# A two-layer RWKV-7 / gMLP trunk: a third plain pair in the first FFN, four weight splits moved from GpSimd to VectorE, and group norm's root by ScalarE

## The chip, the cores and the metric

The kernel runs on one core of a Trainium2 chip. A core has a matrix engine (TensorE, PE in the profile, with its weight loads as PEld), a vector engine (VectorE, DVE), an activation engine (ScalarE, ACT), GpSimd (POOL) and a queue engine that issues DMAs (SyncE, SP). The engines run their own instruction streams in order and wait for each other by semaphores. The metric is the device time of one execution in microseconds; lower is better.

## The reference, cut to what matters

Two layers on x (1 x 512 x 1024, float32). Layer 0 mixes with RWKV-7, layer 1 with a spatial gating unit (SGU). After each mixer comes a SwiGLU FFN of inner width 2816, and each sub-layer has a norm ahead and one behind.

```python
def _rmsnorm(x, g):
    y = x32 * lax.rsqrt(jnp.mean(x32 * x32, axis=-1, keepdims=True) + RMS_EPS)
    return (y * g.astype(jnp.float32)).astype(x.dtype)

def _rwkv7_time_mix(x, ...):
    ...
    y = _rwkv7_scan(r_h, decay.reshape(B, T, H, N), k_h, v_h, -kk, kk * a_h)
    mu = jnp.mean(y, axis=-1, keepdims=True)
    var = jnp.mean(jnp.square(y - mu), axis=-1, keepdims=True)
    y = (y - mu) * lax.rsqrt(var + GN_EPS)              # group norm, 16 heads of 64
    y = y * gn_w.reshape(H, N) + gn_b.reshape(H, N)
    y = y + jnp.sum(r_h * k_h * r_k, axis=-1, keepdims=True) * v_h
    return (y.reshape(B, T, D) * g) @ w_o

def _swiglu(x, w_gate, w_up, w_down):
    return (jax.nn.silu(x @ w_gate) * (x @ w_up)) @ w_down

def reference(x, ...):
    for i in range(DEPTH):                              # DEPTH = 2
        h = _rmsnorm(x, norm_gains[i, 0])
        h = _rwkv7_time_mix(h, ...) if i == 0 else _sgu_mixer(h, ...)
        x = x + _rmsnorm(h, norm_gains[i, 1])
        h = _rmsnorm(x, norm_gains[i, 2])
        h = _swiglu(h, ffn_w_gate[i], ffn_w_up[i], ffn_w_down[i])
        x = x + _rmsnorm(h, norm_gains[i, 3])
    return x
```

## The kernel before

**Products.** Every float32 operand of a large product is split in two parts of TensorE's fp32r type: `hi`, a cast by ScalarE (L179), and `lo`, the rest, a subtraction by VectorE (L180). `mm3` (L204) then issues three matmuls for each tile: hi by hi, hi by lo, lo by hi. `weight` loads a weight tile by SP's queue into one of two `wraw` buffers and splits it; with `pool=True` the cast is L195 and the rest is made by GpSimd (L196).

**Order.** The kernel is written as one program; the builder orders the instructions of each engine by a simulated timeline (`schedule_with_timeline_sim=True`), in which program order is the priority. So an instruction can stand ahead of one that is written before it, where the earlier one has to wait. Tiles come from pools with a fixed number of buffers. The pool `s` has 17 slots of 4 KB a partition, the pool `x` has 13: `hT` (8), the FFN's `act` tiles (11), `cc` and the operands of three products lie in `s`; the raw operands, the operands of the other four products and the weight sums lie in `x`.

**RWKV layer.** The work goes in four blocks of 256 features, each through projection (P), decay and key work (E), the front and back of a block inverse (F, B), a scan over 8 chunks (S) and the finish (N), in the order of the list PLAN: all E steps stand ahead of all N steps. In the scan (L1009 to L1024) TensorE, VectorE and ScalarE (su, Y) hand small tiles to each other. The finish is `group_norm` (L1038 to L1046): a mean, a variance by ScalarE's Square (L1042) and a reduction (L1044), then `rsqrt` (L214 to L223), which makes 1/sqrt by an integer guess and three Newton steps, twelve instructions of VectorE on 128x16 or 128x8, and the scaling of Y (L1046). It is called five times: for blocks 0 to 2 on all tokens, for block 3 on each half of them. Then TensorE transposes Y (yt, L1084), VectorE applies gn_w (L1085), TensorE makes the gate, VectorE multiplies (ob, L1089), and `ob` is split for the output projection.

**out_proj.** Output projection, the norm behind it, the residual and the transposes for the next norm. The result has two column halves of four token tiles; `post0` (L309) takes the squares' sum of the first half (L237) and applies the gain, `post1` (L317, L254 to L258, L320) does the same to the second half, takes the root by ScalarE's Sqrt and VectorE's correction, and adds to x. `norm.step` then transposes x (ptr, L267) and writes `hT` with its two parts, by ScalarE (L60) and VectorE (L62). After the RWKV layer (`spare` is set) post0 is called for each token tile just ahead of post1, and at the first of them a Sqrt of one column (L312) has ScalarE load that function's table early. Elsewhere it stands at the last token tile.

**FFN.** The 22 column tiles of gate and up go in 11 pairs. A plain pair (`plain`, L455 to L470) is two tiles by two weights by 8 k-tiles by three matmuls, 512 columns wide (for the first pair of each FFN two times 256); VectorE multiplies by the row of norms (L467) and by the up part (L469), ScalarE does SiLU (L468), GpSimd multiplies by the row again (L470). The other pairs go by a Strassen-like scheme (`Quads`, p1 to p7): seven products of 24 matmuls of 256 columns (R, Q, Z), on sums of weight quarters (`wsum`, L387) and seven prepared operands `bc` (L105 to L127, made by `quads.first` and `quads.second`). PLAIN = 2 pairs of each FFN are plain. They stand ahead, and the seven operands are made beside them. For the first four weight tiles of the first FFN, `weight` is called with `pool=j < 2`; in the second FFN the weights of its first two tiles come ready from the SGU.

```python
yb = plain(0, None)
quads = Quads(self, norm, yb)
quads.first()
for n in range(1, PLAIN):
    plain(n, yb)
p1(PLAIN); p2(PLAIN)
quads.second()
p1(PLAIN + 1); p2(PLAIN + 1)
for n in range(PLAIN, NJ // 2):
    for p in (p5, p6, p7, p3, p4) if n < PLAIN + 2 else (p1, p5, p6, p2, p7, p3, p4):
        p(n)
```

Of the kernel before, what the change touches and what calls it, by code (L numbers as in the profile page):

```python
# [7 lines left out]
F32 = mybir.dt.float32  # L8
F32R = mybir.dt.float32r
I32 = mybir.dt.int32  # L10
AF = mybir.ActivationFunctionType
ALU = mybir.AluOpType

P = 128
# [3 lines left out]
TT = T // P  # L18
# [4 lines left out]
NJ = DFF // P  # L23
RMS_EPS = 1e-6
GN_EPS = 64e-5
# [10 lines left out]
XV = "xxxessss"  # L36
XSLOTS = 13
LAG = 2
PLAIN = 2
DECAY = 0.5 * 0.6065306597126334  # L40


# [88 lines left out]
class Trunk:  # L131
# [77 lines left out]
    def rsqrt(self, ss, n, scale, eps):  # L209
# [13 lines left out]
            v.scalar_tensor_tensor(y, t, 1.5, y, op0=ALU.add, op1=ALU.mult)  # L223
        return y

    def bcast_row(self, row):

        t = self.gp.tile([P, D], F32, name="gain", tag="gain", bufs=2)
        self.nc.gpsimd.dma_start(out=t, in_=row.partition_broadcast(P))
        return t  # L230
# [42 lines left out]
    def out_proj(self, acts, wrows, nk, row, xts, store=None, tail=3, norm=None, spare=None, mid=None, after=()):  # L273


        nc = self.nc
        v = nc.vector
        gain = self.bcast_row(row)
        nu = nk // 2
        cols = [slice(0, 512), slice(512, 1024)]  # L280
        late = (1, 1) if spare else (0, tail)
        accs, f0, part = [None, None], [], []

        def mms(half, k, tt, w):
            tok = slice(tt * P, (tt + 1) * P)
            hi, lo = acts(k)
            self.mm3(accs[half][tt], (hi[:, tok], lo[:, tok]), w, k == 0, k == nk - 1)

        def unit(half, u):
            own = spare if half and u < nu - late[1] else None  # L290
            with ExitStack() as order:
                for ins in after:
                    order.enter_context(self.tc.issue_after(ins.ins))
                hi, lo = self.weight(wrows(u)[:, :, cols[half]], spare=own)
            return [(2 * u + j, (hi[:, j, :], lo[:, j, :])) for j in range(2)]

        def first(half):
            accs[half] = self.accs(half)
            for u in range(nu - late[half]):
                for k, w in unit(half, u):  # L300
                    for tt in range(TT):
                        mms(half, k, tt, w)

        def post0(tt, junk):
            acc = accs[0][tt]
            s = self.sumsq(acc, junk)
            if tt % 2 == 0:
                f0.append(self.f0p.tile([P, 2, 512], F32, name="f0", tag="f0", bufs=2))
            v.tensor_tensor(f0[-1][:, tt % 2, :], acc, gain[:, cols[0]], op=ALU.mult)  # L309
            part.append(self.part(s, 1.0 / D, RMS_EPS))  # L310
            if tt == (0 if spare else TT - 1):
                nc.scalar.activation(junk[:, 0:1], part[tt][0], AF.Sqrt)  # L312

        def post1(tt, hn):
            acc, lo, hi = accs[1][tt], hn[:, 0:512], hn[:, 512:1024]
            s = self.sumsq(acc, lo)
            v.tensor_tensor(hi, acc, gain[:, cols[1]], op=ALU.mult)  # L317
            y = self.rsqrt1(s, part[tt], 1.0 / D)
            for f, c in ((f0[tt // 2][:, tt % 2, :], cols[0]), (hi, cols[1])):
                v.scalar_tensor_tensor(xts[tt][:, c], f, y[:, 0:1], xts[tt][:, c], op0=ALU.mult, op1=ALU.add)  # L320
                if store is not None and tt == TT - 1:
                    nc.sync.dma_start(out=store[tt * P:(tt + 1) * P, c], in_=xts[tt][:, c])
            if store is not None and tt < TT - 1:
                nc.sync.dma_start(out=store[tt * P:(tt + 1) * P, :], in_=xts[tt])

        hn_tile = lambda: self.sm.tile([P, D], F32, name="hn", tag="hn", bufs=2)
        first(0)
        if not spare:
            for tt in range(TT):
                post0(tt, hn_tile()[:, 0:512])  # L330
        if mid:
            mid()
        first(1)
        ends = [[kw for u in range(nu - late[half], nu) for kw in unit(half, u)] for half in range(2)]
        for tt in range(TT):
            for half in range(2):
                for k, w in ends[half]:
                    mms(half, k, tt, w)
            if norm and tt >= LAG:
                norm.step(tt - LAG, xts[tt - LAG])  # L340
            hn = hn_tile()
            if spare:
                post0(tt, hn[:, 512:1024])
            post1(tt, hn)
        if norm:
            for tt in range(TT - LAG, TT):
                norm.step(tt, xts[tt])
            norm.finish()
# [5 lines left out]
    def ffn(self, li, xts, norm, store=None, nxt=None, early=()):  # L354
        nc = self.nc
        early = list(early)
        v, a = nc.vector, nc.scalar
        gains = self.i["norm_gains"]
        wgu = self.gate_up(li)
        wd = self.i["ffn_w_down"][li].rearrange("(u j p) n -> u p j n", p=P, j=2)  # L360
        hT, b = norm.hT, {}
        acts, pairs, loads, seeded = [], {}, [0], []
# [27 lines left out]
        def p1(n):  # L390
            o = pairs[n] = dict(act=self.slot([P, 2, T], F32, "act"))
            acts.append(o["act"])
            o["a11"] = quad(n, 0, 0)
            o["R"] = self.bank("R", "R")
            product(o["R"], 1, o["a11"], True)
            if len(seeded) < 2:
                q = self.bank("Q", "Q")
                seeded.append(q)
                bh = b[1][0]
                nc.tensor.matmul(q, bh[:, 0, 0:P], bh[:, 0:2].rearrange("p k t -> p (k t)"), start=True, stop=True)  # L400
            o["Q"] = seeded[(n - PLAIN) % 2]
            a.copy(o["Q"], o["R"])

        def gate(dst, src, sign=1.0):
# [7 lines left out]
        def p2(n):  # L412
            o = pairs[n]
            o["a12"] = quad(n, 1, 0)
            product(o["R"], 2, o["a12"])
            gate(o["act"][:, 0, g], o["R"])
# [36 lines left out]
        def plain(n, yb):  # L453
            act = self.slot([P, 2, T], F32, "act")
            acts.append(act)  # L455
            for f in range(2):
                j = 2 * n + f
                ws = early.pop(0) if early else [self.weight(w[:, :, j * P:(j + 1) * P], pool=j < 2) for w in wgu]
                pp = [self.bank("gu", "gu") for _ in range(2)]
                for c in ((g, u) if j < 2 else (slice(0, 512),)):  # L460
                    for w, ps in zip(ws, pp):
                        for kt in range(KT):
                            self.mm3(ps[:, c], (w[0][:, kt, :], w[1][:, kt, :]), (hT[kt][:, 0, c], hT[kt][:, 1, c]),
                                     kt == 0, kt == KT - 1)
                yb = norm.row() if yb is None else yb
                t = act[:, f]
                v.tensor_tensor(t, pp[0], yb, op=ALU.mult)  # L467
                a.activation(t, t, AF.Silu)  # L468
                v.tensor_tensor(t, t, pp[1], op=ALU.mult)  # L469
                nc.gpsimd.tensor_tensor(t, t, yb, op=ALU.mult)  # L470
            return yb
# [2 lines left out]
        quads = Quads(self, norm, yb)  # L474
        b = quads.b
        quads.first()
        for n in range(1, PLAIN):
            plain(n, yb)
        p1(PLAIN)
        p2(PLAIN)  # L480
        quads.second()
        p1(PLAIN + 1)
        p2(PLAIN + 1)
        for n in range(PLAIN, NJ // 2):
            for p in (p5, p6, p7, p3, p4) if n < PLAIN + 2 else (p1, p5, p6, p2, p7, p3, p4):
                p(n)

        halves = {}
# [41 lines left out]
    def rwkv(self, x0):  # L530
# [3 lines left out]
        with ExitStack() as ctx:  # L534
# [496 lines left out]
            def group_norm(Y, tts):  # L1031

                n, n4 = len(tts), 4 * len(tts)
                ts = slice(tts[0], tts[-1] + 1)
                y4 = Y[:, ts].rearrange("p t q (h v) -> p (t q h) v", h=2)
                yf = Y[:, ts].rearrange("p t q f -> p (t q f)")
                mu = self.sm.tile([P, n4], F32, name="mu", tag="mu", bufs=2)
                v.tensor_reduce(mu, y4, axis=mybir.AxisListType.X, op=ALU.add)  # L1038
                v.tensor_scalar(mu, mu, 1.0 / 64, None, op0=ALU.mult)
                v.tensor_tensor(y4, y4, mu.unsqueeze(2).broadcast_to([P, n4, C]), op=ALU.subtract)  # L1040
                sq = self.sm.tile([P, n4, C], F32, name="hn", tag="hn", bufs=2)
                a.activation(sq.rearrange("p q v -> p (q v)"), yf, AF.Square)  # L1042
                va = self.sm.tile([P, n4], F32, name="va", tag="va", bufs=2)
                v.tensor_reduce(va, sq, axis=mybir.AxisListType.X, op=ALU.add)  # L1044
                rs = self.rsqrt(va, n4, 1.0 / 64, GN_EPS)
                v.tensor_tensor(y4, y4, rs.unsqueeze(2).broadcast_to([P, n4, C]), op=ALU.mult)  # L1046

            def bonus(b, o):
# [244 lines left out]
```

## Time and profile before

| | us |
|---|---|
| median of 3 runs (lowest, highest) | 1354.4 (1348.42, 1357.36) |
| the profiled execution: time, span | 1345.89, 1344.2 |
| mean granted clock of TensorE | 0.979 |
| first FFN: first gate/up matmul, first R, last Q | 466.2, 519.9, 712.5 |
| second FFN: first R, last Q | 1033.9, 1219.4 |
| TensorE busy in 320 to 340, 360 to 380, 400 to 420 | 16.47, 15.61, 20.00 |

The span is from the first to the last instruction. A row of a timeline gives the start, the duration, the engine, the line, the operation, the tiles written and read, the shapes and the count; in brackets stand the engine's idle time ahead of it and what ended it. Busy times of TensorE are modelled, since matmuls are pipelined: 0.28 us stands for a 256-column matmul of which the next one starts after 0.12 us. So work is counted by matmuls and stretches. PEclk is the clock granted to TensorE, 1.00 for full speed. The lines that carry the argument are shown in the prediction.

### The profile page before, as it was taken

The page shows a single profiled execution, that of the slowest core. Times are in us where ns is not written, and L with a number is a line of the kernel's source. Part 1 is how long each engine was busy: PE and PEld are TensorE (multiplying, and loading weights), DVE is VectorE, ACT ScalarE, POOL GpSimd, SP SyncE. Part 2 cuts the span into 40 slices and gives each one's busy share as a digit, 9 for nine tenths or more (in the row PEclk, how much of TensorE's full clock was granted, in tenths as well). Part 3 has the DMA queues.
Part 4 walks back from the last instruction along what each step waited for, and adds up shares of the span by engine and source line. Part 5 has one row for each costly group of instructions (what it writes and reads, how often), then busy time and mean ns, then how long its engine had stood idle before and what let it go on. Part 6 is the DMA issues. An engine that isn't in the chain of part 4 may idle for free.

```text
span 1344.2 us, 24525 instructions
## 1 busy us (share of the span) xinstructions
PE 1279.7 (95%) x9812; PEld 1115.3 (83%) x9812; DVE 898.5 (67%) x1520; ACT 694.9 (52%) x1240; POOL 166.3 (12%) x306
## 2 busy tenths in 40 slices
PE   5999999988989799999999999999999999999997
PEld 3677799887767698899998887878888999998886
DVE  7975846667856589778775325575689878785223
ACT  7976884757443554445454314543464455464221
POOL 0000373665000121000000002020002000000000
PEclk9999999989889999999999999999999999999999
DMA  5146683412143233333323332343430443323231
GB/s 159 47 107 169 165 199 127 123 47 78 45 139 106 72 91 101 107 114 108 106 87 110 94 112 91 93 140 98 142 95 2 125 126 95 97 78 125 94 94 63
DMA packets 217266, 140.10 MB, mean 104 GB/s; under 512 B 67856, under 2 KB 193344, under 8 KB 217152
## 3 DMA queue, kind: packets, MB, share of 16 engines
q1 hardware_dynamic: 215856, 133.81, 34.6%
q0 software_dynamic: 1296, 4.72, 1.0%
q8 instruction: 77, 1.26, 0.4%
q14 instruction: 37, 0.30, 0.1%
HBM read 124.35 MB, written 14.16 MB: 103 GB/s over the span
## 4 chain that ended last, share of the span: by engine, by line
PE 58%; DVE 5%; ACT 1%; issue 1%; DMA 0%; SPq 0%; DVEq 0%; ACTq 0%
PE acc L204 24%; PE Q L204 11%; PE Z L204 7%; PE R L204 7%; PE gu L204 5%; PE u L204 3%; DVE wlo L180 1%; DVE wsum L387 1%; PE s L1227 1%; PE ptr L267 0%; ACT whi L179 0%; DVE braw L106 0%; DVE hT L62 0%; DVE bc L180 0%; DVE x L320 0%
## 5 line engine op out<-in xcount | busy, mean ns | idle before, releaser
L180 DVE TENSOR_TENSOR wlo<-wraw,whi 128x1024 fp32r<-128x1024 f32 x109 | 133.6, 1226 | 197.8 <-ACT whi L179 197.4
L179 ACT CAST whi<-wraw 128x1024 fp32r<-128x1024 f32 x109 | 114.2, 1048 | 224.1 <-PE acc L204 140.9
L204 PE MATMUL acc<-whi,actw 128*128 128x512 f32 x704 | 220.7, 394 | 0.0
L204 PE MATMUL Q<-bc,whi 128*128 128x256 f32 x864 | 157.2, 282 | 3.5 <-ACT hn L431 2.2
L204 PEld LDWEIGHTS acc<-whi,actw 128*128 128x128 f32 x704 | 132.3, 188 | 30.7
L204 PE MATMUL acc<-wlo,actw 128*128 128x512 f32 x352 | 138.7, 394 | 0.0
L204 PEld LDWEIGHTS Q<-bc,whi 128*128 128x128 f32 x864 | 133.8, 190 | 4.3 <-ACT hn L431 2.6
L179 ACT CAST whi<-wsum 128x1024 fp32r<-128x1024 f32 x72 | 75.2, 1050 | 90.3 <-PE Q L204 31.3
L204 PE MATMUL Q<-bc,wlo 128*128 128x256 f32 x432 | 121.7, 282 | 0.0
L204 PE MATMUL Z<-bc,whi 128*128 128x256 f32 x576 | 106.8, 283 | 0.0
L204 PE MATMUL R<-bc,whi 128*128 128x256 f32 x576 | 105.3, 281 | 0.8 <-ACT whi L179 0.8
L180 DVE TENSOR_TENSOR wlo<-wsum,whi 128x1024 fp32r<-128x1024 f32 x72 | 87.0, 1220 | 20.3 <-ACT whi L179 19.1
L204 PE MATMUL gu<-hT,whi 128*128 128x256 f32 (+1 forms) x384 | 91.5, 331 | 5.0 <-DVE hT L62 3.6
L179 ACT CAST whi<-wq 128x1024 fp32r<-128x1024 f32 x54 | 56.6, 1049 | 66.0 <-PE R L204 22.3
L204 PEld LDWEIGHTS R<-bc,whi 128*128 128x128 f32 x576 | 88.9, 188 | 1.3 <-ACT whi L179 1.0
L204 PEld LDWEIGHTS Z<-bc,whi 128*128 128x128 f32 x576 | 89.7, 190 | 0.1
L180 DVE TENSOR_TENSOR wlo<-wq,whi 128x1024 fp32r<-128x1024 f32 x54 | 67.4, 1250 | 28.8 <-ACT whi L179 28.7
L204 PE MATMUL Z<-bc,wlo 128*128 128x256 f32 x288 | 81.4, 283 | 2.3 <-DVE wlo L180 2.3
L204 PE MATMUL proj<-xsp,whi 128*128 128x512 f32 x256 | 82.4, 401 | 1.3 <-ACT r L674 1.3
L204 PEld LDWEIGHTS Q<-bc,wlo 128*128 128x128 f32 x432 | 82.1, 190 | 0.0
L204 PE MATMUL R<-bc,wlo 128*128 128x256 f32 x288 | 81.0, 281 | 0.0
L204 PEld LDWEIGHTS acc<-wlo,actw 128*128 128x128 f32 x352 | 66.0, 188 | 15.3
(346 smaller groups left out, 2841.2 us busy)
## 6 DMA issues: line engine op xcount, KB each, us to landing
wraw<-in_ffn_w_down_dram SPq DMA_DIRECT2D x44, 512.0 KB, 3.7
wq<-in_ffn_w_gate_dram SPq DMA_DIRECT2D x72, 256.0 KB
wq<-in_ffn_w_up_dram SPq DMA_DIRECT2D x72, 256.0 KB, 4.2
wraw<-in_rwkv_w_rkv_dram SPq DMA_DIRECT2D x24, 512.0 KB, 5.4
wraw<-in_sgu_w_in_dram SPq DMA_DIRECT2D x16, 512.0 KB, 4.5
x<-in_x_dram SPq DMA_DIRECT2D x8, 512.0 KB, 3.4
ST<-sb SPq DMA_DIRECT2D x8, 512.0 KB
MV<-sa SPq DMA_DIRECT2D x32, 128.0 KB, 3.5
```

The costliest lines, as they stand in the source:

```text
L179: self.nc.scalar.copy(hi, src)
L180: self.nc.vector.tensor_tensor(lo, src, hi.bitcast(F32), op=ALU.subtract)
L204: self.nc.tensor.matmul(out, l, r, start=start, stop=stop, skip_group_check=resumed)
L387: v.tensor_tensor(s, x, y, op=ALU.add)
L1227: mm(acc[:, tt * P:(tt + 1) * P], vt[tt][:, m * P:(m + 1) * P], wsT[:, m, :], start=True, stop=True)
```

## The change

PLAIN becomes a number for each FFN: three plain pairs in the first, two in the second as before. The first four weight tiles of the first FFN are split as all others are, the second part by VectorE. `group_norm` calls a new `rsqrtn`: five instructions of VectorE and a Sqrt of ScalarE in between. With `spare`, post0 no longer issues the early Sqrt, and its unused output lies in the first half of the tile hn, not the second. The SGU's `weight(..., pool=half == 0)` stays.

```diff
-PLAIN = 2
+PLAIN = (3, 2)
...
+    def rsqrtn(self, ss, n, scale, eps):
+
+        sm, v = self.sm, self.nc.vector
+        c, r, m = (sm.tile([P, n], F32, name=t, tag=t) for t in ("nr_a", "nr_y", "nr_t"))
+        v.tensor_scalar(c, ss, scale, eps, op0=ALU.mult, op1=ALU.add)
+        self.nc.scalar.activation(r, c, AF.Sqrt)
+        v.reciprocal(r, r)
+        v.tensor_tensor(m, r, r, op=ALU.mult)
+        v.scalar_tensor_tensor(m, m, -0.5, c, op0=ALU.mult, op1=ALU.mult)
+        v.scalar_tensor_tensor(r, m, 1.5, r, op0=ALU.add, op1=ALU.mult)
+        return r
...
-            if tt == (0 if spare else TT - 1):
+            if not spare and tt == TT - 1:
                 nc.scalar.activation(junk[:, 0:1], part[tt][0], AF.Sqrt)
...
             if spare:
-                post0(tt, hn[:, 512:1024])
+                post0(tt, hn[:, 0:512])
             post1(tt, hn)
...
+        first = PLAIN[li]
...
-            o["Q"] = seeded[(n - PLAIN) % 2]
+            o["Q"] = seeded[(n - first) % 2]
...
-                ws = early.pop(0) if early else [self.weight(w[:, :, j * P:(j + 1) * P], pool=j < 2) for w in wgu]
+                ws = early.pop(0) if early else [self.weight(w[:, :, j * P:(j + 1) * P]) for w in wgu]
...
-        for n in range(1, PLAIN):
+        for n in range(1, first):
             plain(n, yb)
-        p1(PLAIN)
-        p2(PLAIN)
+        p1(first)
+        p2(first)
         quads.second()
-        p1(PLAIN + 1)
-        p2(PLAIN + 1)
-        for n in range(PLAIN, NJ // 2):
-            for p in (p5, p6, p7, p3, p4) if n < PLAIN + 2 else (p1, p5, p6, p2, p7, p3, p4):
+        p1(first + 1)
+        p2(first + 1)
+        for n in range(first, NJ // 2):
+            for p in (p5, p6, p7, p3, p4) if n < first + 2 else (p1, p5, p6, p2, p7, p3, p4):
                 p(n)
...
-                rs = self.rsqrt(va, n4, 1.0 / 64, GN_EPS)
+                rs = self.rsqrtn(va, n4, 1.0 / 64, GN_EPS)
```

## The prediction

> **What bounds the kernel now.** I read the page's first part, the busy time by windows, the waits of TensorE, and then each engine's timeline around the three places that the diff touches.
>
> ```profile
> span 1344.2 us, 24525 instructions
> PE 1279.7 (95%) x9812; PEld 1115.3 (83%) x9812; DVE 898.5 (67%) x1520; ACT 694.9 (52%) x1240; POOL 166.3 (12%) x306
> ```
>
> TensorE is busy for 95% of the span, so time can be gained only where it waits, runs at a lower clock, or does work that another form does in less. The two FFNs are the largest stretches, and their Strassen-like parts (from the first R product to the last Q product) hold the same work, 9 pairs of 7 products each. The windows over exactly these two stretches, the first FFN's and then the second's:
>
> ```profile
> core 0: us, PE busy (x) PEld busy (x) DVE busy (x) ACT busy (x) POOL busy (x), PEclk, DMA share, GB/s
> 519.80:712.50 192.70, 187.13 (x1534) 185.15 (x1534) 152.68 (x163) 99.65 (x136) 3.36 (x3) 0.99 0.34 99
> 1033.90:1219.45 185.55, 184.43 (x1533) 183.14 (x1532) 147.59 (x158) 98.88 (x136) 1.89 (x2) 1.00 0.35 100
> ```
>
> With the same matmuls (x1534 and x1533) the first FFN takes 192.70 us and the second 185.55: 7.15 us more. Where they are lost stands in the waits of TensorE between 460 and 580 us and in windows of 10 us (columns as above):
>
> ```profile
> PE gu L204 <- DVE hT L62: 3.3, 1, 3.3
> PE Z L204 <- DVE wlo L180: 2.3, 1, 2.3
> PE gu L204 <- ACT hT L60: 1.4, 1, 1.4
> PE Q L204 <- ACT whi L179: 1.3, 1, 1.3
> PE Q L204 <- ACT hn L431: 1.1, 1, 1.1
> ```
>
> ```profile
> 470.00:480.00 10.00, 10.00 (x67) 10.00 (x68) 10.00 (x35) 7.39 (x25) 4.95 (x3) 0.76 0.45 129
> ...
> 520.00:530.00 10.00, 10.00 (x86) 9.96 (x85) 10.00 (x9) 5.64 (x8) 2.22 (x1) 1.00 0.00 1
> 530.00:540.00 10.00, 7.94 (x64) 7.44 (x62) 7.91 (x9) 4.53 (x7) 0.00 (x0) 1.00 0.38 107
> 540.00:550.00 10.00, 8.39 (x58) 8.40 (x59) 7.81 (x9) 3.20 (x5) 0.00 (x0) 0.83 0.62 171
> ```
>
> VectorE (the third busy time) is busy for all of 520 to 530, with operands of the seven products and the first weight sums at once. Behind that, TensorE's Z and Q wait 2.3 + 1.3 + 1.1 = 4.7 us, and from 540 to 550 it issues 58 matmuls where 520 to 530 has 86, at a granted clock of 0.83. The waits on hT, 3.3 and 1.4 us, belong to the hand-over from out_proj to the FFN.
>
> **The change part by part.** First, the third plain pair of the first FFN. One pair of seven products leaves and one of 96 matmuls of 512 columns comes (2 tiles x 2 weights x 8 k x 3). Both rates are in the chain of waits:
>
> ```profile
> 709.64 2.82 PE Q L204 x24
> 712.46 113.78 PE acc L204 x491
> ```
>
> A product takes 2.82 to 2.88 us in that chain, I take 2.85: 7 x 2.85 = 19.9 us. A 512-column matmul takes 113.78 / 491 = 0.232 us: 96 x 0.232 = 22.2 us. TensorE's own work grows by **+2.3 us**. The bytes are the same (a pair's weights either way), in four DMAs of 512 KB instead of eight of 256 KB on SP's queue, and wq loads come later by one pair.
>
> Against that stands the cover. During 22.2 us more of plain work VectorE has only the pair's own instructions to add:
>
> ```profile
> L180 DVE TENSOR_TENSOR wlo<-wraw,whi 128x1024 fp32r<-128x1024 f32 x4 | 4.9, 1220 | 4.1 <-ACT whi L179 4.0
> L467 DVE TENSOR_TENSOR act<-gu,hn 128x512 f32<-128x512 f32 x4 | 2.7, 680 | 0.0
> L469 DVE TENSOR_TENSOR act<-act,gu 128x512 f32<-128x512 f32 x4 | 2.7, 674 | 0.0
> ```
>
> ```profile
> 512.68 2.21 POOL L470 TENSOR_TENSOR act<-act,hn 128x512 f32<-128x512 f32 x1 [4.03 <-DVE act L469]
> 513.66 2.32 DVE L123 SCALAR_TENSOR_TENSOR braw<-braw 128x1024 f32<-128x1024 f32 x1
> ...
> 516.50 1.21 DVE L127 SCALAR_TENSOR_TENSOR braw<-braw 128x1024 f32<-128x1024 f32 x1
> ```
>
> That is 4.9 us for four splits and 4 x 0.68 = 2.7 us for four products, 7.6 us. The second fence shows a further price: L123 starts within GpSimd's L470 and takes 2.32 us, where L127, the same form beside no GpSimd work, takes 1.21; two more L470 cost VectorE some 2 x 1.1 = 2.2 us. So 22.2 - 7.6 - 2.2 = 12.4 us of VectorE's time are left for a backlog whose visible loss is 7.15 us. I take that the first FFN's loss falls to the second's, **-7.1 us**. Bounds: nothing regained (0), and the whole 7.15 with the 1.1 us wait on hn L431 besides (-8.2). I take the end near the second FFN, because there the same code with the same slots has no such loss, with VectorE less busy (147.59 us).
>
> Second, the hand-over. In out_proj the preload of the Sqrt table in post0 goes, since group norm's Sqrt has loaded it earlier, and its junk moves to the other half of hn (the two Squares are ScalarE's in order, so nothing). Picked from the timelines of ScalarE, VectorE, TensorE and GpSimd there (start, us, engine, line):
>
> ```profile
> 175.64 1.28 ACT L803 ACT_TABLE_LOAD   x1
> 446.64 1.28 ACT L312 ACT_TABLE_LOAD   x1 [0.86 <-DVE rh L245]
> 448.04 0.58 ACT L237 ACTIVATE hn<-acc 128x512 f32<-128x512 f32 x1
> 448.75 0.69 DVE L317 TENSOR_TENSOR hn<-acc,gain 128x512 f32<-128x512 f32 x1 [2.12 <-ACT hn L237]
> 450.26 0.40 DVE L1089 TENSOR_TENSOR ob<-gate,ob 128x256 f32<-128x256 f32 x1
> 451.31 0.21 DVE L257 SCALAR_TENSOR_TENSOR rt<-rr,rm 128x1 f32<-128x1 f32 x1
> 450.72 0.64 PE L1084 MATMUL yt<-ident,Y 128*128 128x128 f32 x2 [2.16 <-DVE ob L1089]
> 451.16 0.80 PE L204 MATMUL acc<-whi,oT 128*128 128x512 f32 x1
> 453.89 0.56 PE L204 MATMUL gate<-sg,g2h 128*128 128x256 f32 x2
> 465.19 2.35 POOL L196 TENSOR_TENSOR wlo<-wraw,whi 128x1024 fp32r<-128x1024 f32 x1 [1.13 <-ACT whi L195]
> 465.54 2.02 DVE L257 SCALAR_TENSOR_TENSOR rt<-rr,rm 128x1 f32<-128x1 f32 x1
> 469.59 2.15 DVE L62 SCALAR_TENSOR_TENSOR hT<-ptr,vecT,hT 128x128 fp32r<-128x128 f32 x8
> ```
>
> The preload holds ScalarE from 446.64 to 448.04; L237 follows, L317 waits for it, L1089 stands behind L317 on VectorE, and TensorE's transposes of yt wait for L1089. Without it this chain starts 448.04 - 446.64 = 1.4 us earlier, and some 0.1 for the wait ahead of it: -1.5 us. Behind the wait the six matmuls from 451.16 to 453.89 take 2.73 us where six at 0.232 take 1.39. The wait left, 2.16 - 1.5 = 0.7 us, is shorter than the 1.3 us one on whi above, which lies in 530 to 540 at clock 1.00 (the 2.3 us wait lies across 540, before the 0.83). So I count the low clock as gone too, 1.3 us and 0.2 for the four gate matmuls behind: together **-3.0 us**. Bounds 0 (hT decides the end of the stage anyway) and -3.0.
>
> [...]
>
> Third, the first four second parts go from GpSimd to VectorE. Each takes GpSimd 2.35 us in the row above and VectorE 1.22. GpSimd's first one ran while VectorE waited; its second lies over L257, which takes 2.02 us where the one at 451.31 takes 0.21: -1.8 us on the path L257, x, hT L62, behind which TensorE waits 3.3 us. In exchange VectorE gets four times 1.15 (1.22 less the overlap of neighbours). I take one of the four ahead of hT and the others in its gaps and behind it: -1.8 + 1.15 = **-0.7 us**. Bounds: -1.8 (none ahead) and 4 x 1.15 - 1.8 = +2.8 (all ahead).
>
> Fourth, group norm's root. Twelve instructions of VectorE become five and a Sqrt of ScalarE, at five places. The last of them:
>
> ```profile
> 435.80 0.17 DVE L223 SCALAR_TENSOR_TENSOR nr_y<-nr_t,nr_y 128x8 f32<-128x8 f32 x1
> 436.00 0.69 DVE L1046 TENSOR_TENSOR Y<-Y,nr_y 128x512 f32<-128x512 f32 x1
> 443.51 0.38 PE L1084 MATMUL yt<-ident,Y 128*128 128x128 f32 x2
> ```
>
> The last root is done at 436.0 and applied by 436.7; TensorE takes it up at 443.51, 6.8 us later, behind its own work. So this one gains nothing. The steps are 0.2 us apart (435.80 to 436.00), so each place frees 7 x 0.2 = 1.4 us of VectorE, and the first adds one table load of 1.28 us on ScalarE (no other set is loaded between 175.64 and 446.64, and the functions used in between run on the table at hand, so one load does for all). I take **-1.0 us**; bounds -7.0 (5 x 1.4, all on the path) and, above nothing, the rival below.
>
> The sum: 2.3 - 7.1 - 3.0 - 0.7 - 1.0 = -9.5 us. The profiled run took 1345.89 us, so the like of it would take 1336.4. It lies 8.5 us below the median of the three runs, 1354.4, and below the lowest of them, 1348.42; against the median the forecast is 1354.4 - 9.5 = 1344.9 us.
>
> **The rivals.** (a) The loss in the first FFN moves along with the Strassen part. For it: the operand of the fifth product and the act tiles need room that hT holds until the last plain matmul, with three plain pairs as with two, and the loads of the next weights wait for weight sums. Against it: the second FFN has the same slots and does not lose there. Then -7.1 falls away: 1354.4 - 2.4 = 1352.0 us. (b) The second parts crowd VectorE at the hand-over, all four ahead of hT. For it: VectorE is busy 10.00 of 10 us from 470 to 480. Then the preload's gain waits for hT too, and the sum is 2.3 - 7.1 + 2.8 - 1.0 = -3.0: 1351.4 us. [...] (d) VectorE paces the recurrence, and its freed time counts in full: -7.0 in place of -1.0, 1338.9 us. (e) Slower: Sqrt stands in ScalarE's queue behind copies of the scan that wait for VectorE and TensorE, and VectorE's next steps wait for the root.
>
> ```profile
> ACT su L1014 <- DVE su L1011: 8.6, 5, 3.8
> ACT Y L1024 <- PE Yp L1022: 8.3, 4, 6.9
> ```
>
> Between 380 and 470 us such a wait is 3.8 us at its longest for su and 6.9 for Y. Five roots that each cost 3.8 us are 19 us: -8.5 without the fourth term, so +10.5, 1364.9 us. It decides from 8.5 / 5 = 1.7 us for each root on. Against it: the mean of these waits is 1.7 and 2.1 us, and the last root has 6.8 us to spare.
>
> **How the numbers follow.** Forecast 0.42; (a) 0.20, (b) 0.13, (c) 0.06, (d) 0.12, (e) 0.07. A measurement of this kernel can tell about 1%, 13.5 us, from no change. Faster by more than that takes (d), 0.12, and the upper edge of the forecast with runs that spread by 9 us, 0.08: 0.20. Slower by over 1% needs most of (e) and an unlucky median: 0.04. Within 1%: 0.76. The range takes in (d) with the spread of runs below it and (a) and (b) above: 1336 to 1354 us; (e) and the far ends are left out.
>
> **What would show it.** Right: the stretch from the first R to the last Q holds 8 pairs in about 165 us (185.55 - 19.9), with no wait of Z on wlo and clock 1.00; no table load near 447 and one near 288; yt waiting under 1 us; L257 at 0.2 us; TensorE's wait on hT L62 shorter than 3.3 us. Wrong: Z, Q and R wait some 5 us again behind the third pair; VectorE's wlo standing between L257 and L62 with a longer wait on hT; TensorE idle on Y's scaling with Sqrt behind su or Y on ScalarE; or a shift in the recurrence, whose order of instructions may come out anew, of more than the 1 us that I give it.

## The result and the profile after

| | before | after |
|---|---|---|
| median of 4 runs each (lowest, highest), us | 1351.41 (1348.23, 1357.36) | 1333.93 (1329.93, 1341.57) |
| ratio after / before, 95% interval | | 0.9876 [0.9843, 0.991] |
| profiled execution: time, span, us | 1345.89, 1344.2 | 1336.29, 1334.6 |

The changed kernel is some 17 us faster, where 9.5 were forecast; its median lies below the range. By the ratio it is 1.2% faster (interval 0.9 to 1.6), and 1.3% in a second series (e1 below, 1.05 to 1.56): more than the bound of 1%, to which 0.2 was given. The two profiled executions are only 9.6 us apart. That of before is a low draw: in 121 later runs of that kernel, of median 1349.6, only 8 were lower. Runs in a slow state stand in no ratio here: four of before's 125 later ones (1365.8 us and more) and one of e14's. The span cut into stages, by the first and last instructions of each (us; the last Q by its start):

| stage | before | after | difference |
|---|---|---|---|
| start to the first group norm's mean | 278.5 | 281.3 | +2.8 |
| from there to the first gate/up matmul (recurrence, out_proj, norm) | 187.7 | 179.9 | -7.8 |
| plain pairs of the first FFN | 53.7 | 74.6 | +20.9 |
| first R to last Q of the first FFN | 192.3 | 164.6 | -27.7 |
| from there to the end | 632.0 | 634.2 | +2.2 |

The first and the last stage have the same work in both. A second profile of the changed kernel (e1) has 278.1 us in the first, and the last takes 631.9 to 634.8 in all traces below whose second FFN takes 184 to 186 us: so I take these two differences for the draw. What is left is 20.9 - 27.7 = -6.8 us for the third pair and -7.8 us ahead of the FFN. These -14.6 us and the draw's +5.0 make the 9.6 between the profiles. So it is luck that the forecast for a run like the profiled one, 1336.4, is what the profiled run took, 1336.29. The windows of after over the Strassen-like stretch of the first FFN and over that of the second:

```profile
core 0: us, PE busy (x) PEld busy (x) DVE busy (x) ACT busy (x) POOL busy (x), PEclk, DMA share, GB/s
535.80:700.40 164.60, 163.52 (x1363) 162.30 (x1362) 131.71 (x141) 88.56 (x122) 2.42 (x3) 1.00 0.36 103
1025.20:1210.10 184.90, 183.83 (x1532) 182.47 (x1531) 147.27 (x157) 98.59 (x135) 1.89 (x2) 1.00 0.35 100
```

The stretch of eight pairs takes 164.6 us, one pair (19.9) less than the second FFN's nine, at clock 1.00: the 7 us that the first FFN had lost are gone. The waits of TensorE in after from 446 to 760 us show the same:

```profile
engine line waited for: us in total, times, longest us
PE ptr L279 <- DVE hT L62: 1.6, 2, 1.1
PE Q L204 <- ACT hn L444: 1.1, 1, 1.1
PE gu L204 <- DVE hT L62: 1.1, 2, 0.8
PE gu L204 <- ACT hT L60: 1.0, 1, 1.0
PE acc L204 <- ACT oT L179: 0.7, 1, 0.7
```

No Z waits for wlo any more, and the wait of gu for VectorE's hT has gone from 3.3 to 1.1 us, while the transposes ptr now wait for it for 1.6 us. Picked from the timelines of ScalarE, TensorE and VectorE in after:

```profile
287.71 1.28 ACT L231 ACT_TABLE_LOAD   x1
444.67 0.44 PE L1097 MATMUL yt<-ident,Y 128*128 128x128 f32 x2 [0.79 <-DVE ob L1102]
462.52 0.21 DVE L269 SCALAR_TENSOR_TENSOR rt<-rr,rm 128x1 f32<-128x1 f32 x1
```

The table is loaded once, in the first group norm; yt waits 0.79 us instead of 2.16; the small correction (L257 before, L269 now) takes 0.21 us, with no split of GpSimd beside it; before's 2.02 us began within one of 2.35. These signs came as forecast. The recurrence did not. VectorE's rows in the two kernels, before and then after, from the first group norm's mean to the third block's Qs (in brackets the idle time ahead):

```profile
278.46 1.22 DVE L1038 TENSOR_REDUCE mu<-Y 128x16 f32<-128x1024 f32 x1
314.43 1.92 DVE L916 STREAM_TRANSPOSE Dt<-Dm 128x1024 f32<-128x1024 f32 x1
324.26 0.69 DVE L935 TENSOR_TENSOR Qs<-Qp,id 128x512 f32<-128x512 f32 x1 [0.16 <-PE Qp L932]
```

```profile
281.28 1.22 DVE L1051 TENSOR_REDUCE mu<-Y 128x16 f32<-128x1024 f32 x1
313.77 1.92 DVE L929 STREAM_TRANSPOSE Dt<-Dm 128x1024 f32<-128x1024 f32 x1
317.76 0.69 DVE L948 TENSOR_TENSOR Qs<-Qp,id 128x512 f32<-128x512 f32 x1 [0.76 <-PE Qp L945]
```

From the mean to Dt (both inputs of the block inverse are transposed there) before needs 36.0 us and after 32.5; from Dt to Qs 9.8 and 4.0. Between the two lie block 2's Qp products on TensorE. Here are the rows of Qp and of the scan's step (us) there, in before and in after (the trace counts each of these small matmuls twice: block 2's 64 are 80 + 10 + 18 + 20 = 128 in after):

```profile
314.97 0.32 PE L932 MATMUL Qp<-hn,LA 32*32 32x32 f32 x14
315.22 0.45 PE L1009 MATMUL us<-su,MV 128*64 128x64 f32 x8
315.71 0.37 PE L932 MATMUL Qp<-hn,LA 32*32 32x32 f32 x18
...
318.92 0.45 PE L1009 MATMUL us<-su,MV 128*64 128x64 f32 x8
319.42 0.45 PE L932 MATMUL Qp<-hn,LA 32*32 32x32 f32 x30
320.88 0.39 PE L932 MATMUL Qp<-hn,LA 32*32 32x32 f32 x24
323.32 0.45 PE L1009 MATMUL us<-su,MV 128*64 128x64 f32 x8
323.81 0.38 PE L932 MATMUL Qp<-hn,LA 32*32 32x32 f32 x22
```

```profile
313.97 0.89 PE L945 MATMUL Qp<-hn,LA 32*32 32x32 f32 x80
315.40 0.31 PE L945 MATMUL Qp<-hn,LA 32*32 32x32 f32 x10
316.73 0.37 PE L945 MATMUL Qp<-hn,LA 32*32 32x32 f32 x18
317.33 0.38 PE L945 MATMUL Qp<-hn,LA 32*32 32x32 f32 x20
```

Before, three scan steps stand among the Qp in TensorE's queue, and the last of the Qp come behind them, at 323.81. After, the Qp stand together. No line of the diff says so: the builder planned the queue anew for the shorter root (e5 below, without the root, has TensorE's queue of before). So two theories stood for the recurrence: "VectorE's time" (the seven freed instructions at each root count) and "order" (the new queue counts).

### The profile page after: what moved, and what is told of

It reads as the page before. It is cut to its first block, busy times and chain, and to the rows that moved or that the text cites. A ratio compares the mean times of both kernels' runs of the same rounds, so it can differ in the third digit from the quotient of the medians.

```text
span 1334.6 us, 24342 instructions
## 1 busy us (share of the span) xinstructions
PE 1281.5 (96%) x9740; PEld 1112.1 (83%) x9740; DVE 885.4 (66%) x1481; ACT 690.0 (52%) x1237; POOL 160.7 (12%) x304
## 4 chain that ended last, share of the span: by engine, by line
PE 66%; DVE 6%; ACT 2%; DMA 2%; issue 2%; POOL 1%; SPq 0%; DVEq 0%; ACTq 0%; POOLq 0%
PE acc L204 27%; PE Q L204 10%; PE gu L204 9%; PE R L204 7%; PE Z L204 7%; PE u L204 3%; DVE wlo L180 1%; PE gh L993 1%; DMA wraw<-in_rwkv_w_o_dram 1%; ACT hn L249 1%; ACT whi L179 1%; PE s L1240 1%; DVE wsum L400 0%; DVE tm L923 0%; ACT hT L60 0%
## 5 line engine op out<-in xcount | busy, mean ns | idle before, releaser
L180 DVE TENSOR_TENSOR wlo<-wraw,whi 128x1024 fp32r<-128x1024 f32 x117 | 144.9, 1238 | 194.8 <-ACT whi L179 194.3
L179 ACT CAST whi<-wraw 128x1024 fp32r<-128x1024 f32 x117 | 122.6, 1049 | 236.1 <-PE acc L204 143.1
L204 PE MATMUL Q<-bc,whi 128*128 128x256 f32 x816 | 147.4, 281 | 2.2 <-ACT hn L444 2.2
L204 PEld LDWEIGHTS Q<-bc,whi 128*128 128x128 f32 x816 | 125.6, 189 | 2.7 <-ACT hn L444 2.6
L204 PE MATMUL gu<-hT,whi 128*128 128x256 f32 (+1 forms) x448 | 112.8, 344 | 2.3 <-ACT hT L60 1.2
L204 PE MATMUL Q<-bc,wlo 128*128 128x256 f32 x408 | 114.6, 281 | 0.0
L204 PE MATMUL Z<-bc,whi 128*128 128x256 f32 x544 | 99.6, 281 | 0.0
L204 PE MATMUL R<-bc,whi 128*128 128x256 f32 x544 | 98.9, 281 | 0.0
L204 PEld LDWEIGHTS gu<-hT,whi 128*128 128x128 f32 x448 | 79.4, 199 | 12.6 <-ACT hT L60 1.9
L179 ACT CAST whi<-wq 128x1024 fp32r<-128x1024 f32 x51 | 53.5, 1049 | 68.4 <-PE gu L204 20.9
L204 PEld LDWEIGHTS Z<-bc,whi 128*128 128x128 f32 x544 | 84.0, 189 | 0.0
```

What stands on the lines that cost most here:

```text
L179: self.nc.scalar.copy(hi, src)
L180: self.nc.vector.tensor_tensor(lo, src, hi.bitcast(F32), op=ALU.subtract)
L204: self.nc.tensor.matmul(out, l, r, start=start, stop=stop, skip_group_check=resumed)
```

## The experiments

Each ratio is to the kernel before, timed on the same chip, with its 95% interval; 0.001 is 1.35 us. The last four columns are from each run's trace (us): from the first group norm's mean to the third block's Qs and to the first gate/up matmul, and from the first R to the last Q of each FFN (the first FFN has nine pairs there, or eight, marked *).

| run | ratio | to Qs | to gate/up | FFN 1 | FFN 2 |
|---|---|---|---|---|---|
| before | 1 | 45.8 | 187.7 | 192.3 | 185.5 |
| e1 changed kernel again | 0.987 [0.9844, 0.9895] | 36.9 | 181.1 | 164.6* | 184.7 |
| e2 third pair alone | 1.0017 [0.9994, 1.0039] | 45.8 | 189.9 | 170.5* | 185.4 |
| e3 second parts alone | 0.9976 [0.9949, 1.0002] | 45.8 | 186.8 | 191.6 | 185.4 |
| e4 root and preload | 0.9899 [0.9875, 0.9923] | 36.9 | 180.1 | 188.2 | 185.0 |
| e5 preload alone | 0.9981 [0.9957, 1.0004] | 46.2 | 187.4 | 192.4 | 185.5 |
| e6 without root and preload | 0.9968 [0.9939, 0.9998] | 44.9 | 187.7 | 165.5* | 185.3 |
| e7 without second parts | 0.9922 [0.9892, 0.9952] | 36.6 | 177.7 | 164.6* | 191.1 |
| e8 without third pair | 0.9891 [0.9859, 0.9924] | 36.4 | 178.7 | 190.0 | 185.1 |
| e9 root, VectorE padded | 1.004 [1.0014, 1.0066] | 46.6 | 191.0 | 188.5 | 185.0 |
| e10 root, GpSimd padded | 0.9983 [0.9968, 0.9998] | 43.8 | 185.8 | 189.9 | 185.0 |
| e11 old root, B2 earlier | 1.0071 [1.0052, 1.0089] | 31.5 | 195.3 | 190.1 | 189.2 |
| e12 changed kernel, B2 earlier | 0.9984 [0.9965, 1.0003] | 32.4 | 192.4 | 164.9* | 184.7 |
| e13 new root, Qp cut up | 1.0066 [1.0039, 1.0094] | 44.5 | 193.1 | 191.9 | 191.3 |
| e14 old root, Qp together | 1.0012 [0.9989, 1.0035] | 39.5 | 189.2 | 190.0 | 185.3 |
| e15 changed kernel, Qp in one piece | 0.9968 [0.9941, 0.9995] | 35.6 | 190.2 | 165.3* | 189.5 |
| e16 old root, e4's queue | 1.008 [1.0049, 1.0112] | 40.4 | 191.3 | 192.3 | 190.4 |
| e17 new root, before's queue | 1.0039 [1.0019, 1.0059] | 46.0 | 194.0 | 189.7 | 192.4 |
| e18 e5 with e4's queue | 1.0044 [1.0021, 1.0067] | 40.5 | 189.1 | 189.0 | 191.5 |

**The changed kernel again, and each part alone (e1 to e5).** e2 to e4 apply one part of the diff shown above to the kernel before: PLAIN = (3, 2); `weight` without `pool=j < 2`; `rsqrtn` with the early Sqrt left out and its junk moved. e5 keeps the old root; the early Sqrt goes, and the first group norm loads the table with a Sqrt of one column:

```diff
+                if not inv2:
+                    inv2.append(1)
+                    a.activation(self.small("rr"), va[:, 0:1], AF.Sqrt)
```

> The changed kernel once more, five rounds against the kernel before, since the two profiled executions differ by 9.6 us (1344.2 to 1334.6) but the medians by 17.5. Theory A (the profiled execution of the kernel before was an early one among its runs, and the change is worth more in a typical run): ratio 0.986 to 0.990, and the profiled spans differ by 13 us or more. Theory B (the sum of -9.5 us is the worth of the change, and the first medians were an uneven draw): ratio 0.992 to 0.995.

> Only the third plain pair in the first FFN, all else as before. By the forecast's terms +2.3 - 7.1 = -4.8 us, ratio 0.9965, with the stretch from the first R to the last Q at 165 us. Rival (the loss moves along with the Strassen part): +2.3 us, ratio 1.002, and that stretch at 172 us. Rival of theory A: this part carries the missing 7 us, ratio 0.991 or less.

> Only the four second parts by VectorE instead of GpSimd. By the forecast's terms -0.7 us, ratio 0.9995; L257 near 466 us takes 0.2 us. Rival (they crowd VectorE ahead of hT): +2.8 us, ratio 1.002, with a longer wait of TensorE on hT. Rival of theory A: VectorE's blocked time counts in full (L257 and L105, 4 us), ratio 0.997.

> Only group norm's root by ScalarE, with the early Sqrt of post0 left out and its junk moved. By the forecast's terms -3.0 - 1.0 = -4.0 us, ratio 0.997. Rival (VectorE paces the recurrence and its freed time counts in full): -10 us, ratio 0.9926, with the first matmul of the FFN 8 us or more earlier. Rival (Sqrt stands behind the scan's copies): slower, ratio 1.005 or more.

> The kernel before with its Newton root, but the early Sqrt of post0 left out, its junk moved, and one Sqrt of one column issued in the first group norm instead (block 0), so that the table is loaded there. VectorE, TensorE and the queues keep the order of the kernel before. Root alone measured 0.9899 (-13.6 us) where I had -3.0 for the hand-over and -1.0 for the root. Theory A (the hand-over was mis-sized: the low clock and what hangs on it are worth more): -8 us or more, ratio 0.994 or less. Theory B (the hand-over is worth its 3.0 us, and the recurrence the rest): ratio 0.9978, yt waiting under 1 us, first matmul of the FFN 3 us earlier than in the kernel before.

The root and the preload bring 13.6 us, the preload alone 2.6 (its interval reaches just past none), so the root some 11 us. The second parts bring 3.2 (not told from none). The third pair alone brings nothing, and its stretch keeps 5 us of the loss that the changed kernel has not. VectorE's rows in e2 and in after at that place show why:

```profile
559.72 2.36 DVE L388 TENSOR_TENSOR wsum<-wq 128x1024 f32<-128x1024 f32 x2 [1.53 <-DMA wq<-in_ffn_w_up_dram]
562.00 1.22 DVE L388 TENSOR_TENSOR wsum<-wsum,wq 128x1024 f32<-128x1024 f32 x1
563.13 1.22 DVE L180 TENSOR_TENSOR bc<-tsum,bc 128x1024 fp32r<-128x1024 f32 x1
```

```profile
546.93 1.22 DVE L400 TENSOR_TENSOR wsum<-wsum,wq 128x1024 f32<-128x1024 f32 x1
548.07 1.22 DVE L180 TENSOR_TENSOR bc<-tsum,bc 128x1024 fp32r<-128x1024 f32 x1
549.20 2.35 DVE L400 TENSOR_TENSOR wsum<-wq 128x1024 f32<-128x1024 f32 x2
```

In e2 the two sums of weight quarters stand ahead of an operand that is ready (bc, whose cast by ScalarE ends at 557.8), wait 1.53 us for their load and hold bc up; in after bc stands first and nothing waits. A Z of e2 then waits 2.5 us for wlo, as before. The work is the same; the builder's order differs. The five other traces with three pairs (e1, e6, e7, e12, e15) have the order of after there, and no Z in that stretch waits more than 0.4 us. That the order makes the loss rests on these seven traces; no run changed it alone.

**One part left out (e6 to e8).** The changed kernel without the root and the preload (e6), without the second parts (e7), and with PLAIN = 2 for both (e8).

> The changed kernel without group norm's new root and with the early Sqrt back in post0: third plain pair and second parts by VectorE. The sum of the two measured alone is 1.0017 and 0.9976, -1 us: ratio 0.9993. Theory A (the third pair pays only where VectorE reaches the Strassen part free of the hand-over's stalls): the stretch from the first R to the last Q falls from 170.5 us (third pair alone) to 165 and the ratio to 0.995. Theory B (it takes the root's new order, not the second parts): the stretch stays at 170 us and the ratio at 0.999.

> The changed kernel with the first four second parts back on GpSimd: third plain pair and the new root. Theory A (second parts by VectorE bring the Strassen part to 165 us): that stretch is 170 us, L257 or its like is blocked for 2 us again, and the ratio is 0.9916. Theory B (they are worth 0.7 to 3 us at the hand-over only): the stretch is 165 us and the ratio 0.988 to 0.989.

> The changed kernel with two plain pairs in the first FFN: new root and second parts by VectorE. If the third pair is worth the forecast's 4.8 us in this company, ratio 0.9905 (0.987 + 0.0035). If it is worth nothing, as alone (1.0017), ratio 0.985 to 0.987 and this is the fastest version. The stretch from the first R to the last Q with 9 pairs: 188 us as with the root alone, or 185.5 as in the second FFN.

Against e1 the root and the preload are worth (0.9968 - 0.987) x 1350 = 13.2 us, the second parts 7.0 and the third pair 2.8 (not told from none: the two intervals together leave 5 to 6 us to each side). Of the second parts' 7.0, 6.4 lie in the second FFN, which that edit does not touch: 191.1 us for 184.7. Its waits from 1020 to 1235 us in e7, and its windows there:

```profile
PE Z L204 <- DVE wlo L180: 2.9, 1, 2.9
PE Q L204 <- ACT hn L444: 1.8, 2, 1.1
```

```profile
1050.00:1060.00 10.00, 7.08 (x52) 6.88 (x51) 7.30 (x8) 3.38 (x5) 0.00 (x0) 0.89 0.60 161
1060.00:1070.00 10.00, 10.00 (x82) 10.00 (x81) 4.79 (x6) 3.67 (x5) 0.00 (x0) 0.94 0.03 7
```

It is a loss like that of the first FFN, now at the second: Z waits for wlo, and the clock is at 0.89 and 0.94 in the two windows from that wait on. Seven of the nineteen traces in the table have 189 to 192 us there, each with a wait of Z of 2.6 to 2.9 us: for wlo in e7, e13, e17 and e18, for the operand bc in e11, e15 and e16. The others have 184 to 186 and no such wait.

**VectorE's time or the order: padded roots and another list (e9 to e12).** e9 is e4 with seven idle instructions in the root, which give VectorE back its twelve; in e10 they go to GpSimd. e11 and e12 swap entries of PLAN in the kernel before and in the changed one.

```diff
         v.reciprocal(r, r)
+        for _ in range(7):
+            v.tensor_scalar(r, r, 1.0, None, op0=ALU.mult)
```

```diff
-... S1 F3 N0 B2 N1 ...
+... S1 B2 N0 F3 N1 ...
```

> The new root with the early Sqrt left out, and seven idle instructions of VectorE (r times 1) in each root, so that VectorE has twelve again and a Sqrt besides. The planned order has block 2's 64 Qp matmuls cut up by three scan steps, as before (11 steps ahead of the first, 14 ahead of the last), where the new root without the seven has them together (11 and 11). Theory 'order' (the gain of the root is the place of the Qp in TensorE's queue): only the preload's 2.6 us, ratio 0.998, first gu at some 467 us, the third block's Qs some 45 us behind the first group norm's mean. Theory 'VectorE's time' (the seven freed instructions count): the same here, since VectorE has them back: 0.998. Theory 'neither' (the Sqrt itself, the table or the early load bring it): 0.990, gu at 459.

> As the run before, but the seven idle instructions go to GpSimd: VectorE has its five, so all of its time is freed, while the order of TensorE's queue stays the old one (11 and 14). The root itself takes longer from mean to scaling. Theory 'order': no gain beyond the preload, ratio 0.998 or above, first gu at 467 us or later, third block's Qs at +45. Theory 'VectorE's time': most of the root's gain stays, 0.990 to 0.993, first gu at 459 to 462.

> The kernel before with its Newton root and early Sqrt; in the list PLAN, B2 stands ahead of N0 and F3, so that block 2's Qp matmuls stand together (11 and 11) though VectorE has all twelve instructions. Theory 'order': 8 to 10 us faster, ratio 0.993, first gu some 8 us ahead of that of the kernel before, third block's Qs at +37 rather than +46. Theory 'VectorE's time': no change, ratio 1.000, gu at 467.

> The changed kernel with the same list as the run before (B2 ahead of N0 and F3). Block 2's Qp stand together in both; block 3's come two scan steps later than in the changed kernel (19 for 17). Theory 'order': as the changed kernel within 3 us, ratio 0.985 to 0.989 to the kernel before. Theory 'VectorE's time': the same, since nothing of VectorE changes: the run looks for a faster version, and does not tell the two apart.

e10 has VectorE's time free and the Qp cut up, and gains no more than the preload: against "VectorE's time", though its root also takes longer (at block 0 7.8 us from the first instruction to the scaling of Y, 1.4 in e4). e9 is slower than before, which neither theory had. e11 has the third block's Qs 14.3 us earlier with the old root, but not by the Qp alone: 8.9 of them lie ahead of Dt (27.1 us behind the mean for 36.0), with N0's root behind it on VectorE, and 5.4 between Dt and Qs, where the Qp now stand together. N0 and F3 moved behind B2, and the fourth block and the finish lost more than that. "Order" in its simple form (Qp together, so 8 us faster) falls. e12 was no faster version.

**Only the Qp moved (e13 to e15).** e13 is e4 with the Qp held behind the steps that cut them up before; e14 is the kernel before with a high priority on block 2's Qp, and e15 the changed kernel with it.

```diff
+                    with ExitStack() as cut:
+                        if b == 2 and u >= 2:
+                            cut.enter_context(self.tc.issue_after(self.cuts[0 if u < 6 else 1 if u < 13 else 2].ins))
...
+                with (self.tc.high_priority() if b == 2 else ExitStack()):
```

> The new root with the early Sqrt left out (as in e4), and block 2's Qp matmuls cut up as in the kernel before: 8 after the 11th scan step, 16 more after the 12th, 28 after the 13th and 12 after the 14th, by an order on TensorE's queue alone. Up to the first Qp the order is that of e4. Theory 'order': the third block's Qs comes some 6 us later than in e4 (+43 us behind the first group norm's mean rather than +37), the ratio to the kernel before is 0.994 to 0.998, first gu at 464 to 468 us. Theory 'VectorE's time': as e4, 0.990, gu at 459.

> The kernel before with its Newton root and its early Sqrt; only block 2's 64 Qp matmuls are given a high priority, so that they stand together behind the 11th scan step. Up to the first Qp the order is that of the kernel before. Theory 'order': the third block's Qs 6 us earlier (+40 rather than +46), ratio 0.994 to 0.996, first gu 5 to 7 us earlier. Theory 'VectorE's time': 1.000, gu at 467.

> The changed kernel with the same high priority: its Qp stood together but for eight small matmuls of other work and one Yp between them; now all 64 are in one piece, and the builder plans what follows anew. Both theories: as the changed kernel within 4 us, ratio 0.984 to 0.990; the run looks for a faster version.

The third block's Qs follows the Qp as "order" said: 44.5 with the new root cut up, 39.5 with the old one together. The end does not follow. In e14 the 6.3 us gained there are 1.1 at the fourth Qs (87.7 us behind the mean, 88.8 before), and none at the first gate/up matmul; in e13 TensorE's queue behind the fourth Qs is planned otherwise and needs 107.0 us to the first gate/up matmul, for 99.2 in e4, and the second FFN loses 6 us besides. e15 is slower than the changed kernel.

**Root and queue set apart (e16 to e18).** TensorE's instructions, from the middle of the recurrence to the first gate/up products, get a fixed order by edges from each to the next, without a wait: e4's order for the old root (e16, and e18 with e5's preload), and the order of before for the new root (e17).

```diff
+    for first, then in zip(todo, todo[1:]):
+        tc.add_manual_dep(then, first.name, info, reason="queue")
```

> The kernel before (Newton root, twelve instructions of VectorE, early Sqrt), with TensorE's queue in e4's order, instruction by instruction, from the middle of the recurrence to the first FFN's first gate and up products; the other engines' order is the builder's. Theory 'order': most of the gain comes with the queue alone, 6 to 9 us: ratio 0.993 to 0.996, first gu at 459 to 462 us (some +181 behind the first group norm's mean). Theory 'VectorE's time': no gain, 0.999 or above; TensorE waits in its new order where VectorE is late, gu at 466 or later.

> The new root with the early Sqrt left out (as e4), with TensorE's queue in the order of the kernel before over the same stretch. Theory 'order': the preload's 2.6 us and the 3 us by which VectorE is earlier at the third block's Dt, no more: ratio 0.995 to 0.998, gu at 463 to 466. Theory 'VectorE's time': most of e4's gain stays, 0.990 to 0.993, gu at 459 to 461.

> As e16, with the early Sqrt left out of out_proj and the table loaded in the first group norm (as e5). It differs from e4 by the twelve instructions for five and a Sqrt alone, at one order of TensorE's queue. Theory 'order': 0.991 to 0.994. Theory 'VectorE's time': 0.998, as e5.

With the early Sqrt out in all four, ratio and time from the mean to the first gate/up matmul are:

| | queue of before | queue of e4 |
|---|---|---|
| old root | 0.9981, 187.4 (e5) | 1.0044, 189.1 (e18) |
| new root | 1.0039, 194.0 (e17) | 0.9899, 180.1 (e4) |

Both theories fall. The shorter root alone loses 6.6 us in this stretch, the queue alone 1.7, and both together gain 7.3. (The ratios of e17 and e18 also hold 6 to 7 us of the second FFN; e16, with the early Sqrt in, takes 191.3 us.) In e4's queue the root is worth 189.1 - 180.1 = 9.0 us, in the old queue -6.6. Of the 9.0 us, 4.7 are idle time of TensorE (20.4 us in e18, 15.7 in e4) and 4.3 longer busy time, at a mean clock of 0.91 in e18 and 0.94 in e4. The largest waits of TensorE in e18 from 300 to 445 us that e4 has not:

```profile
PE Q2p L955 <- ACT Dn L947: 2.4, 1, 2.4
PE Qp L932 <- DVE hn L915: 2.3, 1, 2.3
PE us L1009 <- DVE MV L982: 1.8, 2, 1.5
PE yt L1089 <- DVE Y L1051: 1.3, 1, 1.3
```

With the old root VectorE is late for Qp, for two scan steps and for yt, and ScalarE for Q2p, and a queue in fixed order has nothing else to issue meanwhile. But that is not the root's twelve instructions alone: only TensorE's queue is fixed, and the builder ordered VectorE's anew. The rows at the longest wait for MV, first e4's and then e18's:

```profile
347.62 0.42 DVE L995 TENSOR_TENSOR MV<-gh,MV 128x256 f32<-128x256 f32 x1
347.95 2.11 DVE L927 STREAM_TRANSPOSE hn<-Dm 128x1024 f32<-128x1024 f32 x1
349.92 1.95 DVE L928 STREAM_TRANSPOSE Dt<-Dm 128x1024 f32<-128x1024 f32 x1
```

```profile
351.06 2.10 DVE L915 STREAM_TRANSPOSE hn<-Dm 128x1024 f32<-128x1024 f32 x1
353.02 1.91 DVE L916 STREAM_TRANSPOSE Dt<-Dm 128x1024 f32<-128x1024 f32 x1
354.77 0.41 DVE L982 TENSOR_TENSOR MV<-gh,BX 128x256 f32<-128x256 f32 x1
355.24 0.33 PE L1009 MATMUL us<-su,MV 128*64 128x64 f32 x2 [1.52 <-DVE MV L982]
```

In e18 the two transposes, 3.7 us together, stand ahead of MV, which in e4 stands ahead of them, and TensorE waits 1.52 us for it. So the new queue of TensorE pays where VectorE is in time for it; how much of the 9.0 us is the root's own time, how much VectorE's order and how much the clock is not told apart.

## Why the prediction was wrong, point by point

- **The third pair, +2.3 and -7.1.** Right in company: 164.6 us and no wait of Z, 165 forecast; both terms together -2.8 by runs (-6.8 between the two profiles), -4.8 forecast. The reason given (cover for VectorE's backlog) was only half of it: e2 has that cover and keeps 5 us of the loss, with bc behind two weight sums. The 1.1 us wait of Q on hn, which the prediction counts among the first FFN's loss, stands in the second FFN of every trace too. Rival (a) is what the third pair does alone.
- **The hand-over, -3.0.** Measured -2.6 (e5), interval about 3 us to each side, so not told from none; in e5's one trace the stretch ahead of the first gate/up matmul is 0.3 us shorter (187.4 for 187.7). yt waits less, as forecast (1.15 us in e5). The clock's half of the term (1.5 us) is not borne out. Here are the windows at and behind yt's wait in before (2.16 us), in e3, which has the same wait of 2.16, and in e1 (0.79, and 0.74 of the next product):

```profile
448.00:452.00 4.00, 1.84 (x9) 1.34 (x8) 3.25 (x13) 2.75 (x10) 0.00 (x0) 0.85 0.00 1
452.00:456.00 4.00, 4.00 (x20) 3.33 (x20) 3.17 (x9) 0.14 (x1) 0.00 (x0) 0.72 0.49 135
```

```profile
450.00:454.00 4.00, 1.83 (x10) 1.21 (x9) 3.56 (x15) 2.45 (x9) 0.00 (x0) 1.00 0.09 10
454.00:458.00 4.00, 4.00 (x25) 3.45 (x24) 3.93 (x12) 1.82 (x7) 0.00 (x0) 1.00 0.35 125
```

```profile
440.00:444.00 4.00, 2.47 (x12) 1.69 (x11) 4.00 (x15) 2.57 (x9) 0.00 (x0) 0.90 0.30 90
444.00:448.00 4.00, 4.00 (x16) 3.34 (x15) 2.83 (x11) 0.40 (x1) 0.00 (x0) 0.67 0.12 47
```

  The same wait left the clock at 1.00 in e3 and was followed by 0.72 in before; the short waits of the changed kernel were followed by 0.67 in e1 and by 1.00 in after (0.79 and 0.73 us, and 1.00 from 440 to 460). So the clock here does not go with this wait, and rival (c) (0.06), that the low clock behind yt stays, came in one of the two traces of the changed kernel. What sets it stays open.
- **The second parts, -0.7.** The signs came (0.21 us, the wait on hT at 1.1); alone they measure -3.2, not told from -0.7. Rival (b) did not come.
- **The root, -1.0: the step that failed.** By e4 and e5 it is worth some -11 us (4 to 5 us to each side), in their traces -7.3 ahead of the FFN and -4.2 in the first FFN's Strassen stretch, which is ordered otherwise in e4 (188.2 us for 192.4). The forecast priced five times seven instructions in the queue as it stood, and named a new order in the recurrence only among the things that would prove it wrong. Rival (d) had nearly this size, -7.0, but for another reason: freed time that counts in full. It does not: in the old queue the same root loses 6.6 us. Rival (e) did not come in the changed kernel. e17, where the new root makes the kernel slower, has that sign, but not for that reason: Sqrt starts there 0.03 to 0.49 us behind its input at the five roots.
- **The base.** The forecast took the median of three runs, 1354.4; 121 later runs of that kernel give 1349.6. The sum of -9.5 would have given 1340.1 on that base, inside the range but still 6 us too high.

By runs in company or alone the parts come to -2.8 (third pair, e8), -2.6 (preload, e5), -3.2 (second parts, e3) and -8.9 for the root as the rest of 17.5; each has 3 to 6 us of uncertainty.

Open remains how much VectorE's own queue, left to the builder in e16 to e18, has of the 9.0 and the -6.6; a run with both queues fixed was not tried. That 4 to 7 us in the second FFN come and go with edits far ahead of it is shown; which step of the builder's timeline turns them was not followed.

## What to carry to other kernels

Where a builder orders the queues by a simulated timeline, a small edit has two prices: that of its instructions in the old order, and that of the new order, here 9.0 us gained or 6.6 lost, where the first had been put at 1.0 gained. Ahead of a forecast, compare the two kernels' queues, and widen the range where they part early in a chain of dependent steps. An order that is good for one set of durations can be bad for another: carry over both, or neither.

## What the runs showed of the hardware

In e7 a wait of 2.9 us of Z on wlo comes with a second FFN's stretch that is 6.4 us longer (191.1 for 184.7 in e1). An estimate from its rows: 2.9 us are the wait, 0.7 a second wait on hn (1.8 for the 1.1 of the others) and 1.7 the clock (0.89 and 0.94 over 10 us each, that is 1.1 and 0.6); 1.1 are not placed. In these traces the length of a wait did not by itself tell whether the clock fell: a wait of 2.7 us of Z in the second FFN of e11 left it at 1.00 from 1055 to 1075 us, and 2.16 us of yt was followed by 0.72 in before and by 1.00 in e3.
